# A list scheduler's model that books GpSimd and two-tensor VectorE steps as exclusive, with measured step lengths

## The chip, the cores and the metric

The kernel runs on one core of a Trainium2 chip. The metric is the time of one execution in microseconds, the median of several. Five engines matter. TensorE (PE in the profile; PEld is its weight load) does the matrix products, VectorE (DVE) and GpSimd (POOL) work element by element, ScalarE (ACT) does activations and scaled copies, and SyncE (SP) issues the DMAs. Matmul results land in PSUM banks; all else lies in SBUF.

## The reference

The input is one sequence of 512 tokens of width 2048 with a context of 256 tokens, all in float32. A first block normalizes both, projects them, and runs four attention mixers of four heads (A global, B neighbourhood, C window with sinks, D with low-rank keys and values). A second block has two layers: an even one (causal pooling, and an attention of 16 heads of 64 over the 128 best keys of each query) and an odd one (32 heads of 64 in a window, with sinks).

```python
# first block
h_x = rms_norm(x, norm_g) * (1 + sc_x) + sh_x
px, pc = split_cols(h_x @ w_in), split_cols(h_c @ w_in)
oa, ob, oc, od = mixer_a(...), mixer_b(...), mixer_c(...), mixer_d(...)
x = x + gt_x * (concatenate([oa, ob, oc, od]) @ w_out)
# even layer
h = rms_norm_2(x, norm_g) @ w_in
py = silu(p_gate) * (einsum(pooled, pool_w) * pool_scale)
o = dsa_attention(q, k, dv, iq, ik, iw, rel_bias, topk)   # score + bias, masked, softmax, @ v
x = x + concatenate([py, silu(d_gate) * o]) @ w_out
# odd layer
o = swa_sink_attention(q, k, v, sinks, rel_bias)
x = x + (silu(gate) * o) @ w_out
```

## The kernel before

Activations lie with the 2048 features in 16 tiles of 128 partitions and the tokens in the columns. Every weight and activation is split into a high part (ScalarE, a rounded copy) and a low part (what is left, by VectorE or GpSimd), and a product is three matmuls: high by high, high by low, low by high (L491 to L493, 512 columns each). Weights are streamed from HBM in units of 128 x 512: the load, the high part (L554), the low part (L564, a choice of VectorE or GpSimd) and the matmuls. So one tile of a projection is four units, 48 matmuls (16 feature tiles by three) into one PSUM tile `px`, with 512 tokens as columns.

All work is written as generators, and a list scheduler (`Sched`, L46 to L175) sets the order at build time. Each generator yields an engine and a cost before it issues an instruction. The scheduler keeps a clock for each engine, takes the pending step that could start first by these costs, and emits it. A list of two engines, as `[D(n), G(n, bias=SLACK)]`, leaves the choice to it: the one that would end first, GpSimd with a bonus. The costs are four one-line functions (`D`, `A`, `G`, `M`) and `DC`. What comes out is one fixed order of instructions for each engine. On the chip each engine runs its own list in order and waits only for data and buffers.

The projections have a low priority, so their matmuls fill the times in which attention waits. Where a layer ends, three steps meet. Outputs `o` of heads that were stored in DRAM are loaded again (`reload`, L970) and split at L291 (`o<-b`); the output projection (`out_proj`, L1560) starts its first tiles early, as far as outputs are ready; and the last head's softmax and product (PV) run. A softmax group computes scores `S` for 128 queries, VectorE scales them and adds a bias, ScalarE takes exponentials, the result `P` is scaled (L314 on VectorE or L312 on ScalarE), transposed on TensorE (`T`, L398), split into `pt`, and multiplied with the values.

Names that the steps below use: in the heads of the even and the odd layer (`pair64`, L1748) the bias sum L1803 (`P<-tab,sco` or `P<-tab,cmask`), the score matmuls L1809 and L1810, and the step L1815 that frees the one `S` bank; `rsqrt` (L347), whose last six steps (L363 to L365, twice) are small VectorE steps, booked as one; L412, the matmul of a head's statistics, ahead of those; L1704, which multiplies the result with a row statistic; L1902 and L1904, the PV products there; L1909 to L1921, from PV to the head's output `o`. In the first block, `attention` has the scores at L1113, the scaling of `S` into `P` at L1152, and `k` scaled at L846.

## Time and profile before

| | |
|---|---|
| median of 3 runs | 2746.86 us (2741.91 to 2751.96) |
| the profiled execution's own time | 2743.26 us |
| its span, first to last instruction | 2741.2 us |
| mean granted clock of TensorE | 0.988 |
| busy share of TensorE, VectorE, ScalarE, GpSimd | 97%, 54%, 42%, 40% |
| DMA | 315.98 MB, mean 115 GB/s |

The views are read like this. A wait row names the instruction that waited, what released it, the total wait, how often, and the longest. A timeline row has the start, the duration, the engine, the line, output and inputs, and in brackets how long the engine was idle before it. Engines overlap, so what matters is idle time of TensorE and matmuls at the lower clock (a matmul of 512 columns shows 0.39 us at the full clock, start to start 0.23, and 0.63 at the lower one).

### The profile page before, as it was taken

How to read it: one execution, taken by the hardware profiler on the slowest of the kernel's cores; microseconds unless marked ns; L12 is line 12 of the kernel's file. 1: busy time of each engine (PE TensorE's matmuls, PEld its weight loads, DVE VectorE, ACT ScalarE, POOL GpSimd, SP SyncE). 2: the span in 40 equal slices, each digit the busy share in tenths (PEclk: the TensorE clock that was granted, in tenths of full speed). 3: DMA queues.
4: the chain of work that ended last, by engine and by line, in shares of the span. 5: the costliest groups of instructions: out<-in, count | busy, mean ns of one | idle time of the engine just before them, and what ended most of it. 6: DMA issues, size and time to landing. Idle time of an engine off the chain costs nothing.

```text
span 2741.2 us, 36539 instructions
## 1 busy us (share of the span) xinstructions
PE 2659.6 (97%) x13324; PEld 2189.9 (80%) x13324; DVE 1471.3 (54%) x3242; ACT 1164.1 (42%) x2361; POOL 1098.7 (40%) x886
## 2 busy tenths in 40 slices
PE   7889999999999999999999999999999999999999
PEld 3468888888888887788888878777888888888887
DVE  2457753336552656522368576765215877777500
ACT  3444433333332455433442445454334555555421
POOL 1351333334333333344445544445444333344544
PEclk8989999999999999999999999999999999999999
DMA  9845542222221213244222322224442222222443
GB/s 348 301 166 182 171 144 75 76 72 74 70 71 61 70 65 112 88 144 144 85 85 93 108 85 87 90 78 142 148 140 91 94 87 99 90 80 85 143 139 126
DMA packets 121960, 315.98 MB, mean 115 GB/s; under 512 B 13874, under 2 KB 23986, under 8 KB 121780
## 3 DMA queue, kind: packets, MB, share of 16 engines
q1 hardware_dynamic: 121780, 313.65, 34.4%
q8 instruction: 104, 1.70, 0.3%
q14 instruction: 76, 0.62, 0.1%
HBM read 293.02 MB, written 32.11 MB: 119 GB/s over the span
## 4 chain that ended last, share of the span: by engine, by line
PE 80%; DVE 13%; DMA 2%; ACT 2%; issue 1%; POOL 1%; SPq 0%; DVEq 0%; POOLq 0%; ACTq 0%
PE px L491 20%; PE px L492 20%; PE px L493 20%; PE T L398 4%; PE S L1113 2%; PE pc L496 1%; PE pc L498 1%; PE pc L497 1%; DVE P L1803 1%; DVE P L1815 1%; PE T L412 1%; DVE P L314 1%; PE O L1088 1%; PE O L1089 1%; DVE sm L1820 1%
## 5 line engine op out<-in xcount | busy, mean ns | idle before, releaser
L564 POOL TENSOR_TENSOR w<-wr,w 128x512 fp32r<-128x512 f32 x696 | 919.5, 1322 | 1423.1 <-ACT w L554 1419.0
L554 ACT ACTIVATE w<-wr 128x512 fp32r<-128x512 f32 x736 | 463.2, 630 | 948.4 <-PE px L493 616.0
L491 PE MATMUL px<-u,w 128*128 128x512 f32 x1248 | 498.5, 399 | 0.0
L492 PE MATMUL px<-u,w 128*128 128x512 f32 x1248 | 488.8, 392 | 0.0
L493 PE MATMUL px<-u,w 128*128 128x512 f32 x1248 | 488.4, 391 | 0.0
L491 PE MATMUL px<-hx,w 128*128 128x512 f32 x816 | 331.9, 407 | 9.4 <-ACT w L554 6.3
L492 PE MATMUL px<-hx,w 128*128 128x512 f32 x816 | 323.2, 396 | 2.2 <-POOL hx L291 2.2
L493 PE MATMUL px<-hx,w 128*128 128x512 f32 x816 | 322.3, 395 | 1.7 <-POOL w L564 1.7
L491 PE MATMUL px<-o,w 128*128 128x512 f32 x752 | 295.0, 392 | 3.3 <-ACT o L288 3.3
L492 PE MATMUL px<-o,w 128*128 128x512 f32 x752 | 294.3, 391 | 0.5 <-DVE o L291 0.5
L493 PE MATMUL px<-o,w 128*128 128x512 f32 x752 | 294.0, 391 | 0.0
L493 PEld LDWEIGHTS px<-u,w 128*128 128x128 f32 x1248 | 234.8, 188 | 51.3
L491 PEld LDWEIGHTS px<-u,w 128*128 128x128 f32 x1248 | 236.1, 189 | 40.7 <-issue 0.3
L492 PEld LDWEIGHTS px<-u,w 128*128 128x128 f32 x1248 | 235.7, 189 | 39.6
L291 DVE TENSOR_TENSOR pt<-T,pt 128x512 fp32r<-128x512 f32 (+2 forms) x208 | 127.0, 616 | 111.7 <-ACT pt L288 110.3
L493 PEld LDWEIGHTS px<-hx,w 128*128 128x128 f32 x816 | 154.9, 190 | 38.7 <-POOL w L564 3.3
L491 PEld LDWEIGHTS px<-hx,w 128*128 128x128 f32 x816 | 155.7, 191 | 32.9 <-ACT w L554 9.0
L492 PEld LDWEIGHTS px<-hx,w 128*128 128x128 f32 x816 | 155.7, 191 | 19.8 <-POOL hx L291 2.7
L491 PEld LDWEIGHTS px<-o,w 128*128 128x128 f32 x752 | 142.2, 189 | 33.4 <-ACT o L288 4.0
L492 PEld LDWEIGHTS px<-o,w 128*128 128x128 f32 x752 | 142.1, 189 | 30.5 <-DVE o L291 1.1
L493 PEld LDWEIGHTS px<-o,w 128*128 128x128 f32 x752 | 142.0, 189 | 29.3
L1598 DVE TENSOR_TENSOR xr<-px,xr 128x512 f32<-128x512 f32 x32 | 22.1, 692 | 251.0 <-PE px L493 248.1
(343 smaller groups left out, 4365.2 us busy)
## 6 DMA issues: line engine op xcount, KB each, us to landing
wr<-w SPq DMA_DIRECT2D x237, 512.0 KB, 3.5
wr<-wout SPq DMA_DIRECT2D x89, 512.0 KB, 4.2
wr<-wada SPq DMA_DIRECT2D x37, 512.0 KB, 6.8
gw<-wada SPq DMA_DIRECT2D x64, 256.0 KB, 5.3
wr<-w SPq DMA_DIRECT2D x58, 256.0 KB, 4.0
wr<-wada SPq DMA_DIRECT2D x54, 256.0 KB, 6.0
x<-xr SPq DMA_DIRECT2D x32, 256.0 KB, 4.3
xr<-x SPq DMA_DIRECT2D x32, 256.0 KB, 4.5
```

The source lines that it names most:

```text
L291: eng.tensor_tensor(lo, src, f32(hi), op=OP.subtract)
L314: self.nc.vector.tensor_scalar(dst, src, col, None, op0=OP.mult)
L398: self.nc.tensor.transpose(p[:, j * 128:(j + 1) * 128], x, self.ident)
L412: nc.tensor.matmul(p[:, j * gq:(j + 1) * gq], sq[:, j * 128:(j + 1) * 128], self.ones[:, 0:1] if gq == 1 else self.halves, start=True, sto ...
L491: mm(px, hi[:, s], x[0], **kw)
L492: mm(px, hi[:, s], x[1], start=False, stop=False)
L493: mm(px, lo[:, s], x[0], **ke)
L496: mm(pc, lo[:, s], c[0], **kw)
L497: mm(pc, hi[:, s], c[0], start=False, stop=False)
L554: nc.scalar.activation(w[:, 0], r, AF.Copy)
L564: (nc.gpsimd if e == "POOL" else nc.vector).tensor_tensor(w[:, 1], r, f32(w[:, 0]), op=OP.subtract)
L1113: self.nc.tensor.matmul(o, l, r, start=i == 0, stop=i == len(ops) - 1)
```

## The change

The scheduler's model gets one more resource, `port`. A step whose cost is of the class `Port` can't start before the last such step has ended: all steps of GpSimd, VectorE steps with two operands in SBUF (`D2`, new), VectorE copies in the doubled mode (`x2`) and the small steps `DC`. The constants of the costs change: 0.13 instead of 0.075 us of fixed cost for VectorE, 0.19 instead of 0.1 for ScalarE, 0.15 instead of 0.1 for GpSimd, and 0.4427 ns a column for a matmul instead of 0.4167 and 3 ns. No instruction computes anything else than before; order and choice of engine follow from the costs. The lines move by 15 from L291 on (L291 is L306, L1815 is L1830).

```diff
-    def start(self, t, e):
+    def start(self, t, e, c):
         s = self.engine.get(e, 0.0)
+        if isinstance(c, Port):
+            s = max(s, self.port)
...
             self.engine[e] = end
+            if isinstance(c, Port):
+                self.port = end
...
+class Port(float):
+    pass
...
 def D(n=0, x2=False, k=1, ptr=0):
-    return ("DVE", k * (0.075 + n * (0.52e-3 if x2 else 1.04e-3) + 0.053 * ptr))
+    c = k * (0.13 + n * (0.52e-3 if x2 else 1.04e-3) + 0.053 * ptr)
+    return ("DVE", Port(c) if x2 else c)
+def D2(n=0, k=1, ptr=0):
+
+    return ("DVE", Port(D(n, k=k, ptr=ptr)[1]))
 def DC(k):
 
-    return ("DVE", 0.19 * k)
+    return ("DVE", Port(0.19 * k))
 def A(n=0, ptr=0, acc=0, k=1):
-    return ("ACT", k * (0.1 + n * 0.833e-3 + 0.093 * (ptr + acc)))
+    return ("ACT", k * (0.19 + n * 0.833e-3 + 0.093 * (ptr + acc)))
 def G(n=0, k=1, bias=0.0):
 
-    return ("POOL", k * (0.1 + n * 2.2e-3), bias)
+    return ("POOL", Port(k * (0.15 + n * 2.2e-3)), bias)
 def M(n, passes=1):
-    return ("PE", passes * (n * 0.4167e-3 + 0.003))
+    return ("PE", passes * (n * 0.4427e-3))
...
-            e = yield ([D(n), G(n, bias=SLACK)] if pool else D(n))
+            e = yield ([D2(n), G(n, bias=SLACK)] if pool else D(n))
...
-            e = yield [D(512), G(512, bias=WSLACK)]
+            e = yield [D2(512), G(512, bias=WSLACK)]
...
-                    e = yield [G(n), D(n)]
+                    e = yield [G(n), D2(n)]
```

Some thirty steps are marked in this way. What the order becomes is shown at three places.

VectorE in the second head of the even layer, from the end of its statistics (L1704, now L1719) to the release of the score bank (L1815, now L1830); `tab` and `sco` or `cmask` are the two parts of a bias. Before:

```order
L1704 TENSOR_TENSOR sm_13361<-sm_13361,rt 128x4 x2
L1803 TENSOR_TENSOR P_13433<-tab_13044,cmask 128x128
L1803 TENSOR_TENSOR P_13434<-tab_13044,sco_11354 128x256
L1803 TENSOR_TENSOR P_13433<-tab_13050,cmask 128x128
L1803 TENSOR_TENSOR P_13434<-tab_13050,sco_11354 128x256
L1803 TENSOR_TENSOR P_13435<-tab_13044,sco_11354 128x384
L1803 TENSOR_TENSOR P_13436<-tab_13044,sco_11355 128x512
L924 TENSOR_TENSOR gg_13459<-px_13316,rx 128x512
L1815 SCALAR_TENSOR_TENSOR P_13433<-S_13447,sm_13361,P_13433 128x128
L1803 TENSOR_TENSOR P_13437<-tab_13050,sco_11355 128x512
L1815 SCALAR_TENSOR_TENSOR P_13433<-S_13447,sm_13361,P_13433 128x128
```

Now:

```order
L1719 TENSOR_TENSOR sm_13333<-sm_13333,rt 128x4 x2
L1818 TENSOR_TENSOR P_13419<-tab_13063,cmask 128x128
L1818 TENSOR_TENSOR P_13419<-tab_13067,cmask 128x128
L1926 TENSOR_TENSOR o_13438<-O_13307,b_13437 64x512
L939 TENSOR_TENSOR gg_13449<-px_13280,rx 128x512
L1830 SCALAR_TENSOR_TENSOR P_13419<-S_13444,sm_13333,P_13419 128x128 x2
L1931 TENSOR_TENSOR o_13438<-pc_13327,b_13437 64x512
L1839 TENSOR_REDUCE sm_13466<-P_13419 128x1 x2
```

The sums of 256, 384 and 512 columns no longer stand ahead of the release, and a step of the previous head's output (L1926, once L1911) does. On TensorE, from the statistics (L412) to the second score group, there were 39, 39, 39, 39, 39, 42, 39 and 39 matmuls of projections in the eight heads; now there are 54, 45, 69, 54, 69, 36, 69 and 54. Of the 64 bias sums 15 were on GpSimd, and 32 are now.

VectorE at the end of the first block, the last `rsqrt` (L358 to L365, now L373 to L380) with the split of the last head's values `v` (L291, now L306). Before:

```order
L358 TENSOR_SCALAR sm_9618<-sm_9515 128x6
L291 TENSOR_TENSOR v_9602<-T_9603,v_9602 128x512
L363 TENSOR_TENSOR sm_9618<-sm_9514 128x6
L364 TENSOR_TENSOR sm_9618<-sm_9618 128x6
L365 SCALAR_TENSOR_TENSOR sm_9514<-sm_9618,sm_9514 128x6
L363 TENSOR_TENSOR sm_9618<-sm_9514 128x6
L364 TENSOR_TENSOR sm_9618<-sm_9618 128x6
L365 SCALAR_TENSOR_TENSOR sm_9514<-sm_9618,sm_9514 128x6
L291 TENSOR_TENSOR pt_9627<-T_9610,pt_9627 128x512
```

Now:

```order
L373 TENSOR_SCALAR sm_9608<-sm_9505 128x6
L1054 RECIPROCAL sm_9557<-sm_9557 128x1
L378 TENSOR_TENSOR sm_9608<-sm_9504 128x6
L379 TENSOR_TENSOR sm_9608<-sm_9608 128x6
L380 SCALAR_TENSOR_TENSOR sm_9504<-sm_9608,sm_9504 128x6
L378 TENSOR_TENSOR sm_9608<-sm_9504 128x6
L379 TENSOR_TENSOR sm_9608<-sm_9608 128x6
L380 SCALAR_TENSOR_TENSOR sm_9504<-sm_9608,sm_9504 128x6
L306 TENSOR_TENSOR v_9610<-T_9611,v_9610 128x512
L306 TENSOR_TENSOR pt_9635<-T_9618,pt_9635 128x512
```

The split of `v` has gone behind the six small steps, and the reloaded outputs' splits (`o<-b`) from VectorE to GpSimd, where seven stand in a row (five before).

TensorE in the same stage, at the score groups of the last head (`S<-kvc,qn` and the three rows behind it are one group). Before, the last group:

```order
L491 MATMUL pc_9905<-o_9688,w_9904 128x512
L492 MATMUL pc_9905<-o_9688,w_9904 128x512
L493 MATMUL pc_9905<-o_9688,w_9904 128x512
L1113 MATMUL S_9987<-kvc_9674,qn_9430 128x256 x3
L1113 MATMUL S_9987<-kc_9817,qr_8890 128x256 x2
L1113 MATMUL S_9987<-k_9673,qn_9430 128x512 x3
L1113 MATMUL S_9987<-ks_9816,qr_8890 128x512 x2
L491 MATMUL pc_9905<-o_9705,w_9904 128x512
L492 MATMUL pc_9905<-o_9705,w_9904 128x512
L493 MATMUL pc_9905<-o_9705,w_9904 128x512
L491 MATMUL px_9585<-o_9707,w_9948 128x512
```

Now, the first two groups:

```order
L506 MATMUL px_9586<-o_9787,w_9895 128x512
L507 MATMUL px_9586<-o_9787,w_9895 128x512
L508 MATMUL px_9586<-o_9787,w_9895 128x512
L1128 MATMUL S_9875<-kvc_9819,qn_9416 128x256 x3
L1128 MATMUL S_9875<-kc_9903,qr_8875 128x256 x2
L1128 MATMUL S_9875<-k_9818,qn_9416 128x512 x3
L1128 MATMUL S_9875<-ks_9902,qr_8875 128x512 x2
L1128 MATMUL S_9979<-kvc_9819,qn_9416 128x256 x3
L1128 MATMUL S_9979<-kc_9903,qr_8875 128x256 x2
L1128 MATMUL S_9979<-k_9818,qn_9416 128x512 x3
L1128 MATMUL S_9979<-ks_9902,qr_8875 128x512 x2
L1128 MATMUL S_9995<-kvc_9819,qn_9416 128x256 x3
```

The four groups now follow each other with no matmul of the output projection (`pc<-o`, `px<-o`) between them, and the transposes come right behind; before, 9, 12 and 12 of those matmuls stood between the groups and 12 behind the last.

TensorE at the end of the odd layer, behind the last PV product (L1904, now L1919). Before (`o_22726`, the last head's output, comes 63 matmuls behind the last L1904):

```order
L1902 MATMUL O_22562<-pt_22648,v_2771_17788 128x128
L1904 MATMUL O_22562<-pt_22648,v_2771_17788 128x128
L1902 MATMUL pc_22598<-pt_22648,v_2771_17788 128x128
L1904 MATMUL pc_22598<-pt_22648,v_2771_17788 128x128
L491 MATMUL px_22590<-o_22478,w_22535 128x512
L492 MATMUL px_22590<-o_22478,w_22535 128x512
L493 MATMUL px_22590<-o_22478,w_22535 128x512
L491 MATMUL px_22590<-o_22601,w_22535 128x512
L492 MATMUL px_22590<-o_22601,w_22535 128x512
```

Now, `o_22779` being the last head's output:

```order
L1917 MATMUL O_22655<-pt_22751,v_2772_17800 128x128
L1919 MATMUL O_22655<-pt_22751,v_2772_17800 128x128
L1917 MATMUL pc_22659<-pt_22751,v_2772_17800 128x128
L1919 MATMUL pc_22659<-pt_22751,v_2772_17800 128x128
L506 MATMUL px_22553<-o_22779,w_22684 128x512
L507 MATMUL px_22553<-o_22779,w_22684 128x512
L508 MATMUL px_22553<-o_22779,w_22684 128x512
L506 MATMUL px_22667<-o_22573,w_22706 128x512
L507 MATMUL px_22667<-o_22573,w_22706 128x512
```

The last output is used right behind the last PV; before, 63 matmuls stood between. GpSimd in that stage, before:

```order
L564 TENSOR_TENSOR w_22589<-wr_22476,w_22589 128x512
L291 TENSOR_TENSOR o_22601<-b_22582,o_22601 128x512
L564 TENSOR_TENSOR w_22652<-wr_22476,w_22652 128x512
L291 TENSOR_TENSOR o_22615<-b_22586,o_22615 128x512
L564 TENSOR_TENSOR w_22691<-wr_22554,w_22691 128x512
L291 TENSOR_TENSOR o_22621<-b_22595,o_22621 128x512
L564 TENSOR_TENSOR w_22714<-wr_22554,w_22714 128x512
L564 TENSOR_TENSOR w_22736<-wr_22671,w_22736 128x512
```

Now:

```order
L579 TENSOR_TENSOR w_22595<-wr_22462,w_22595 128x512
L306 TENSOR_TENSOR o_22562<-b_22545,o_22562 128x512
L306 TENSOR_TENSOR o_22564<-b_22546,o_22564 128x512
L306 TENSOR_TENSOR o_22566<-b_22547,o_22566 128x512
L306 TENSOR_TENSOR o_22569<-b_22548,o_22569 128x512
L579 TENSOR_TENSOR w_22634<-wr_22528,w_22634 128x512
L306 TENSOR_TENSOR o_22571<-b_22549,o_22571 128x512
L306 TENSOR_TENSOR o_22573<-b_22550,o_22573 128x512
L306 TENSOR_TENSOR o_22576<-b_22551,o_22576 128x512
L579 TENSOR_TENSOR w_22666<-wr_22528,w_22666 128x512
L306 TENSOR_TENSOR o_22611<-b_22602,o_22611 128x512
```

All eight reloaded outputs are split on GpSimd now, and three were before. Between the even and the odd layer 33 matmuls stood between the last PV and the last output, and 6 do now.

## Rows read from the trace of the kernel before

**Rows 1.** The page: busy time by engine; the granted TensorE clock in 40 slices

```profile
PE 2659.6 (97%) x13324; PEld 2189.9 (80%) x13324; DVE 1471.3 (54%) x3242; ACT 1164.1 (42%) x2361; POOL 1098.7 (40%) x886
...
PEclk8989999999999999999999999999999999999999
```

**Rows 2.** Waits of TensorE, 0 to 200 us (total us, times, longest us)

```profile
PE T L667 <- DMA wr<-wada: 16.3, 6, 7.1
```

**Rows 3.** Waits of TensorE, 1200 to 2741 us

```profile
PE S L1809 <- DVE P L1815: 14.9, 9, 3.0
...
PE px L491 <- ACT o L288: 1.9, 1, 1.9
```

**Rows 4.** Waits of TensorE, 1075 to 1150 us

```profile
PE T L398 <- DVE pt L291: 4.0, 3, 2.8
...
PE T L398 <- DVE v L291: 1.1, 1, 1.1
```

**Rows 5.** Window of the even heads: length, busy us by engine, clock, DMA

```profile
1540.00:1875.00 335.00, 319.99 (x1548) 264.77 (x1548) 247.82 (x499) 168.76 (x369) 154.43 (x131) 0.99 0.26 86
```

**Rows 6.** Timeline of the second even head: start, duration us, instruction, [idle before <-releaser]

```profile
1585.31 0.39 PE L491 MATMUL px<-u,w 128*128 128x512 f32 x1
...
1585.54 0.39 PE L492 MATMUL px<-u,w 128*128 128x512 f32 x1
...
1588.33 1.36 DVE L1704 TENSOR_TENSOR sm<-sm,rt 128x4 f32<-128x4 f32 x2
...
1590.35 1.48 DVE L1803 TENSOR_TENSOR P<-tab,sco 128x256 f32<-128x256 f32 x3
...
1593.73 0.38 PE L1809 MATMUL S<-k,q 128*128 128x256 f32 x1 [3.04 <-DVE P L1815]
...
1595.20 0.63 PE L491 MATMUL px<-u,w 128*128 128x512 f32 x1
...
1595.63 0.63 PE L492 MATMUL px<-u,w 128*128 128x512 f32 x1
```

**Rows 7.** Timeline of VectorE, 1083 to 1096 us, end of the first block

```profile
1085.53 0.68 DVE L291 TENSOR_TENSOR v<-T,v 128x512 fp32r<-128x512 f32 x1
...
1086.88 1.21 DVE L364 TENSOR_TENSOR sm<-sm 128x6 f32<-128x6 f32 x1
...
1091.81 0.17 DVE L365 SCALAR_TENSOR_TENSOR sm<-sm,sm 128x6 f32<-128x6 f32 x1
1091.89 0.68 DVE L291 TENSOR_TENSOR pt<-T,pt 128x512 fp32r<-128x512 f32 x1
```

**Rows 8.** Timeline of GpSimd in the same place

```profile
1085.55 6.21 POOL L291 TENSOR_TENSOR o<-b,o 128x512 fp32r<-128x512 f32 x5 [0.16 <-ACT o L288]
```

**Rows 9.** Timeline, 1131 to 1137 us, behind the last head's scores

```profile
1131.23 0.62 PE L1113 MATMUL S<-ks,qr 128*128 128x512 f32 x2
...
1131.90 1.02 DVE L1152 TENSOR_SCALAR P<-S,sm 128x768 f32<-128x768 f32 x1 [0.36 <-PE S L1113]
...
1135.38 0.62 DVE L314 TENSOR_SCALAR P<-P,sm 128x768 f32<-128x768 f32 x1
...
1136.06 0.77 PE L398 MATMUL T<-ident,P 128*128 128x128 f32 x5 [1.15 <-DVE P L314]
```

**Rows 10.** Timeline, 1893 to 1899 us, the even layer's last output

```profile
1893.23 0.27 PE L1904 MATMUL pc<-pt,v 128*128 128x128 f32 x1
...
1896.93 0.61 ACT L288 ACTIVATE o<-o 128x512 fp32r<-128x512 f32 x1
...
1897.57 1.37 DVE L291 TENSOR_TENSOR o<-o,o 128x512 fp32r<-128x512 f32 x1 [0.91 <-ACT o L288]
```

**Rows 11.** Timeline of GpSimd, 2552 to 2580 us, reloaded outputs

```profile
2564.63 1.29 POOL L291 TENSOR_TENSOR o<-b,o 128x512 fp32r<-128x512 f32 x1 [1.74 <-ACT o L288]
...
2567.58 1.75 POOL L291 TENSOR_TENSOR o<-b,o 128x512 fp32r<-128x512 f32 x1
```

**Rows 12.** Waits of TensorE, 2540 to 2741 us

```profile
PE T L398 <- DVE P L314: 0.2, 1, 0.2
```

More of the change, by code (lines that the diff above doesn't have):

```diff
@@ L75, in __init__ @@
         self.count = 0
+        self.port = 0.0
     def spawn(self, gen, prio=5):
@@ L155, in run @@
                     e, c = t.req[0][:2]
-                    s = self.start(t, e)
+                    s = self.start(t, e, c)
                     fixed.append((e, s, c))
@@ L164, in run @@
                     for e, c, *bias in t.req:
-                        s = self.start(t, e)
+                        s = self.start(t, e, c)
                         f = s + c - (bias[0] if bias else 0)
@@ L279, in spawn, with split @@
         self.s.spawn(gen, prio)
-    def split(self, hi, lo, src, g=None, pool=False, x2=False):
+    def split(self, hi, lo, src, g=None, pool=False, two=False):
         nc = self.nc
@@ L294, in split @@
             nc.scalar.activation(hi, src, AF.Copy, scale=g)
-            yield D(n, ptr=1)
+            yield (D2 if two else D)(n, ptr=1)
             nc.vector.scalar_tensor_tensor(lo, src, g, f32(hi), op0=OP.mult, op1=OP.subtract)
@@ L439, in rope @@
         u = yield from self.alloc("b")
-        yield D(n, ptr=1)
+        yield D2(n, ptr=1)
         nc.vector.scalar_tensor_tensor(dst, src, gain, cos, op0=OP.mult, op1=OP.mult)
@@ L690, in gate @@
                 c = self.csil[:, k:k + 1]
-                yield D(512, ptr=1)
+                yield D2(512, ptr=1)
                 if k == 0:
@@ L742, in stats @@
                 if i > 0:
-                    yield D(n)
+                    yield D2(n)
                     nc.vector.tensor_tensor(sums[0].val, sums[0].val, sums[i].val, op=OP.add)
@@ L825, in q_flow @@
         else:
-            yield from self.split(s[:, 0], s[:, 1], q, self.g(gname))
+            yield from self.split(s[:, 0], s[:, 1], q, self.g(gname), two=True)
             yield ev
@@ L838, in k_norm @@
         if ss_extra is not None:
-            yield D()
+            yield D2()
             nc.vector.tensor_tensor(ss[:, :6], ss[:, :6], ss_extra, op=OP.add)
@@ L928, in silu @@
         nc.scalar.activation(th, px, AF.Tanh, scale=0.5)
-        yield D(512)
+        yield (D2 if rstd is not None else D)(512)
         nc.vector.scalar_tensor_tensor(th, th, 1.0, px, op0=OP.add, op1=OP.mult)
@@ L1035, in soft @@
                 nc.scalar.activation(es, sink, AF.Exp, bias=nm)
-                yield D()
+                yield D2()
                 nc.vector.tensor_tensor(su, su, es, op=OP.add)
@@ L1602, in f @@
                     s = yield from self.pair("u")
-                    yield from self.split(s[:, 0], s[:, 1], xr, self.g(gname, c))
+                    yield from self.split(s[:, 0], s[:, 1], xr, self.g(gname, c), two=True)
                     self.s.set(u[c], (s[:, 0], s[:, 1]))
@@ L1701, in q64 @@
         yield from self.rsqrt(rs, ss, 1.0, EPS * 64)
-        yield D(k=2)
+        yield D2(k=2)
         for i in range(2):
@@ L1838, in soft @@
                 nc.scalar.activation(es, es, AF.Exp)
-                yield D()
+                yield D2()
                 nc.vector.tensor_tensor(su, su, es, op=OP.add)
@@ L1919, in pv_ @@
             th = gev.val
-            yield D(512)
+            yield D2(512)
             nc.vector.scalar_tensor_tensor(o, th, 0.5, o, op0=OP.mult, op1=OP.mult)
@@ L2003, in flow @@
                         count[j] += 1
-                        yield D(n, first)
+                        yield D2(n, first)
                         if first:
@@ L2025, in choose @@
             dg = w[:, j * 128:]
-            yield D(128)
+            yield D2(128)
             nc.vector.tensor_tensor(dg, dg, tri, op=OP.add)
@@ L2071, in flow @@
                 z = two[n % 2]
-                yield D(512)
+                yield D2(512)
                 nc.vector.scalar_tensor_tensor(z, s, 1.0 / w, x, op0=OP.mult, op1=OP.subtract)
                 e = yield from self.alloc("sm")
-                yield D(k=2)
+                yield D2(k=2)
                 nc.vector.tensor_tensor(e[:, :w], s[:, :w], self.rcnt[:, c // 2, :w], op=OP.mult)
```

24 lines of the change are left out of this document (12 added, 12 removed).

## The prediction

> **What bounds the kernel now.** I read the page's shares first: TensorE is busy 97% of the span and the granted clock is full in nearly every slice [rows 1]. No matmul is added or removed, so only idle TensorE time and time at the lower clock can change: 2741.2 - 2659.6 = 81.6 us of idle time, plus the slow stretches. The waits of TensorE, stage by stage, then say whose idle time that is. In the first 200 us it waits mostly for DMA (16.3 us for the modulation weights [rows 2]), and no order of VectorE and GpSimd changes when those bytes land. From 1200 us on one wait stands out: the even layer's score matmul L1809 waits for VectorE to release the only score bank, 14.9 us in 9 waits [rows 3]. At the end of the first block (1075 to 1150 us) the waits are for splits and small steps of VectorE, 4.0 us for split transposes and 1.1 us for a split v [rows 4]. The windows put the even layer's heads at 319.99 us busy of 335 [rows 5].
>
> The timeline of the second even head shows the exclusion that the change is about. A step of two SBUF tensors with 4 columns takes 1.36 us for two [rows 6] while GpSimd runs, and where GpSimd's five splits stand back to back for 6.21 us [rows 8], small steps that take 0.17 us take 1.21 us [rows 7]. The old costs book 0.19 us for such a step and let both engines run at once. So the order is planned on a VectorE that is faster than the real one, and the score bank is released late: 3.04 us of waiting in that head.
>
> **The change part by part.** It adds no instruction to TensorE; it changes the order and which engine takes a split, a bias sum or a scaling. I go by places.
>
> *Even layer, wait for the score bank.* What must be hidden is the chain from the statistics matmul to the second L1815, which releases the bank. In the second head it takes 39 matmuls of 512 columns at 0.227 us (start to start [rows 6]) plus the wait: 8.9 + 3.0 = 11.9 us. The orders give the cover: matmuls between the statistics and the second score group are 39 in seven heads and 42 in one before; now they are 54, 45, 69, 54, 69, 36, 69 and 54. With the chains of before, heads with 54 or more have 12.3 us or more of cover and wait no longer; the second has 10.2 us, but the wide bias sums that stood ahead of its release on VectorE, of which three took 1.48 us [rows 6], are gone from there, so I take no wait; the sixth has 8.2 us and four splits of transposes in its chain, so it still waits some 4 us. Of 14.9 us about 4 stay: -10.9. Bounds: none stays (-14.9); or the 17 bias sums more on GpSimd (15 before, 32 now), at 1.3 us for 512 columns as a split of that size takes [rows 11], hold VectorE back as before (-7).
>
> *Clock.* After the 3.04 us wait the clock drops to its lower level: seven matmuls of 0.63 us, 0.43 apart instead of 0.23 [rows 6], cost 7 x 0.2 = 1.4 us. Two of the nine waits are followed by such a stretch; I take one back: -1.4 (0 to -2.8).
>
> *End of the first block, first part.* Before, v's split comes ahead of the six small steps; it ran just before them, and the split of the transposes came behind at 1091.89 [rows 7]. Now v's split stands behind all six, and GpSimd has seven splits in a row, not five. TensorE's transposed-v work is covered by three matmuls only. v would come up to 1091.9 - 1086.2 = 5.7 us later, of which 2.8 us of the wait for the next split, which falls in the same time, is not paid twice: +3.0 (0 to 5.7).
>
> One rule of the Trainium skill ("SBUF — State Buffer", section "Who interferes with whom") speaks against the change here: the pair of ports that VectorE's second input shares with GpSimd is held by whoever issues first for one whole instruction. The change books six small steps as one hold of 1.14 us; by the rule GpSimd gets in between each two of them, and the trace agrees (at 1086.88 the second step is held for 1.21 us, and the last only begins at 1091.81 [rows 7], beside the 6.21 us of splits [rows 8]). By that the six take some 6 us with seven splits queued, by the booking 1.1 us, and +3.0 would be about 0.
>
> *End of the first block, second part.* The last head's four score groups had 9, 12 and 12 projection matmuls between them and 12 behind; now none. The bank is one: group, then L1152 of 1.02 us, then the next group. A group ends at about 1131.7, L1152 runs from 1131.90 to 1132.92 [rows 9], so each of three gaps is up to 1.3 us; and behind the last group the softmax chain to the scaled P is bare: 1131.7 to 1136.0 is 4.3 us, of which 1.15 was waited before. That is at most 3.9 + 3.2 = 7.1. But the 45 matmuls that left are executed somewhat earlier, where TensorE waited too [rows 4], so part comes back: I take +5 (2 to 7.1).
>
> *Even to odd layer.* From the last PV matmul (1893.5) the hi half of the last output takes to 1897.54 [rows 10]: 4.0 us. Before 33 matmuls cover it, now 6 (1.4 us); 2.6 us come bare, but a wait of 1.9 us for a reloaded output [rows 3] loses its place as 42 instead of 21 matmuls stand ahead of the transposes: +1 (-1 to 3).
>
> *Odd layer to the last projection.* Before, no wait at all worth the name [rows 12]: 63 matmuls between the last PV and the use of the last output. Now none: the whole 4.0 us to hi is bare, plus some 0.2 us to begin. All eight reloaded outputs are now split on GpSimd (three before), five of them in a stretch with only one weight split between. GpSimd gives one per 1.29 to 1.75 us [rows 11], TensorE uses one in three matmuls, 0.68 us; over four in a row 3 x (1.3 - 0.7) = 1.8. Sum +6 (4 to 11, the upper with 1.75 us each and weights' splits late behind them), and one stretch at the lower clock more, +1.4.
>
> *The rest.* Weight splits stay on GpSimd (696 before, 699 now) and are streamed ahead. The scalings moved from VectorE to ScalarE lie on an engine busy 42%. The first 1000 us keep nearly the same order of matmuls; I take 0, with 5 us either way for small shifts.
>
> Sum: -10.9 - 1.4 + 3.0 + 5 + 1 + 6 + 1.4 = +4.1. The profiled execution took 2743.26 us, so 2747.4 by it; the median of the runs is 3.6 us above that execution, so 2751.
>
> **Rivals.** Less than 0.3% (8.2 us) either way is what a measurement of this kernel can't tell from no change.
>
> *The score waits go, the boundaries cost little.* All 14.9 and 2.8 us are won; the projections that were drawn forward fill waits in the places from which the boundaries borrow, so the first block gives +2, the even layer -1, the last +4 as the lower bounds have it: -17.7 + 5 = -12.7, or 2734. For it: the waits at 1083 to 1093 us are there to be filled. Against: the chain behind the last PV can't be hidden without matmuls.
>
> *The boundaries decide.* The price is GpSimd's queue: seven and eight splits in a row in front of which VectorE's small steps stand, at 1.2 us each. From the point where a projection needs a new output every 0.68 us and GpSimd is the only supplier, TensorE goes at GpSimd's pace. Upper bounds of the first block and the last (5.7 + 7.1 + 11), +3 in the even layer, two slow stretches 2.8, against -7 of the score waits and nothing of clock: +22.6, or 2769; half way there it is 2760.
>
> *The change doesn't do what it says.* Nothing on the chip holds the two engines apart: no wait is added between GpSimd and VectorE, so they collide where their data happen to be ready, and the model's reservation is only an order. Then the score chains stay as long as now; the longer cover still works, but the second and the sixth head wait: -9 with no clock won, and the boundaries cost 16.4 as in the sum: +7.4, or 2754. It differs from the forecast in the durations, hardly in the time.
>
> **How the numbers follow.** The forecast's case, boundaries eating up what the score bank gives back, gets 0.40 with the third rival in it, with 2743 to 2758 as its own range; the first rival 0.29, the second 0.31. Faster by over 0.3% is the first rival: 0.29; slower is the second: 0.31; within 0.40. The range goes from 2730, a little under the first rival's time, to 2769, that of the second with its upper bounds.
>
> **What would show it.** Waits of the score matmul on VectorE in the even layer falling from 14.9 to about 4 us, one head carrying nearly all of it, would show the first step. Waits of TensorE at the end of the first block rising from about 9 to about 17 us, with the score matmuls of its last head among them, the second. A wait of about 4 us for the last output right behind the last PV matmul, and GpSimd's splits of reloaded outputs as what is waited for before it, the third. The prediction is wrong if the first 1000 us lose or gain more than 5 us, or if the boundaries show no new wait.

## The result, and the profile after

The changed kernel took 2720.44 us (median of 4, 2719.18 to 2721.56), the kernel before 2747.61 us in the same runs: a ratio of 0.9906, 95% interval 0.9892 to 0.9921. That is 27 us faster, where no measurable change was forecast (2751, range 2730 to 2769). The profiled execution spans 2718.9 us, 22.3 us less than before.

The page of the changed kernel, busy time by engine and the granted clock, against [rows 1]:

```profile
PE 2655.8 (98%) x13324; PEld 2192.5 (81%) x13324; DVE 1362.8 (50%) x3151; ACT 1194.6 (44%) x2415; POOL 1121.8 (41%) x923
...
PEclk8989999999999999999999999999999999999999
```

TensorE idles 63 us (2718.9 - 2655.8) instead of 82. Its waits from 1200 us on (total us, times, longest), against [rows 3]:

```profile
PE px L506 <- ACT o L303: 6.5, 3, 3.3
PE px L507 <- POOL o L306: 1.7, 4, 0.9
PE T L413 <- DVE b L1743: 1.6, 1, 1.6
```

The row of the score matmul is gone altogether: 14.9 us are 0. At its place stand the ends of the layers, waits for the last output and for reloaded ones. The window of the even heads has no idle time left, 377.00 us busy of 377 (columns as in [rows 5]):

```profile
1463.00:1840.00 377.00, 377.00 (x1834) 317.23 (x1833) 237.20 (x522) 189.82 (x400) 212.93 (x189) 1.00 0.29 96
```

To compare two orders, I lined up the two traces by TensorE's own work: its matmuls' columns at 0.4427 ns, 60 ns at least for a matmul, summed up in the order in which they run; both kernels come to 2505 us of it. A stage is a stretch of this sum, and the table gives how long each trace took for the same stretch (from start times of all matmuls; the head counts from the first matmul). The kernels of the experiments below stand in the same table.

| stage (us of work) | before | changed | e1 | e2 | e9 | e10 | e4 | e7 | e12 |
|---|---|---|---|---|---|---|---|---|---|
| head, 0 to 200 | 255.3 | 245.8 | 246.9 | 255.0 | 255.6 | 241.5 | 242.0 | 242.6 | 238.5 |
| first block, 200 to 950 | 809.2 | 801.9 | 802.9 | 808.7 | 807.1 | 800.8 | 802.3 | 801.7 | 802.8 |
| its end, 950 to 1030 | 102.5 | 109.0 | 104.9 | 102.1 | 100.3 | 99.9 | 101.1 | 103.3 | 96.4 |
| even layer, 1030 to 1330 | 307.0 | 308.1 | 307.5 | 308.3 | 314.1 | 305.0 | 308.2 | 306.6 | 307.4 |
| even heads, 1330 to 1680 | 388.0 | 365.9 | 366.0 | 389.6 | 389.0 | 366.1 | 365.9 | 365.9 | 366.0 |
| end of the even layer, to 1722 | 47.3 | 53.1 | 47.0 | 48.5 | 47.2 | 51.9 | 47.7 | 51.4 | 47.2 |
| odd layer, to 2300 | 613.9 | 608.2 | 610.4 | 613.8 | 614.9 | 607.6 | 611.6 | 608.4 | 610.4 |
| its end, to 2360 | 63.8 | 72.7 | 63.7 | 65.0 | 66.5 | 69.3 | 64.8 | 66.9 | 64.0 |

Behind 2360 every trace takes 145 us. Each column is one execution. How far such a stage varies by itself can be read where orders are equal: the head took 245.8, 242.0 and 242.6 us in the changed kernel, e4 and e7, 244.7 and 238.5 in e11 and e12, while the first block behind it agrees within 0.6 us in these groups. So 6 us in the head say nothing; elsewhere it is about 1 us, but more in the even heads where scores wait (see e3).

So the change won 9.5 us in the head, 7.3 in the first block, 22.1 in the even heads and 5.7 in the odd layer, and lost 6.5, 5.8 and 8.9 at the three ends. In the even heads 15.0 of the 22.1 us are idle time (15.0 before, 0 now) and 7.2 are matmuls that took longer around the waits. The granted clock accounts for 3.4 of these: before, it stood at the lower level (0.50) behind the waits of 3.04 and 2.37 us, for 6.8 us together, but not behind one of 3.00 us; now it doesn't fall there. The other 3.8 us fall at the full clock. The head has time at the lower clock as well, a mean granted clock of 0.90 before and 0.93 now, which is 51 and 34 us at half speed (columns as in [rows 5]). The kernel before, its head and the two stretches in the even heads:

```profile
0.00:260.20 260.20, 223.23 (x1092) 145.59 (x1093) 129.75 (x278) 104.07 (x194) 80.47 (x70) 0.90 0.73 254
...
1594.80:1598.20 3.40, 3.40 (x10) 2.72 (x9) 2.31 (x7) 2.42 (x10) 0.62 (x1) 0.50 0.50 158
1772.30:1775.70 3.40, 3.39 (x10) 2.91 (x11) 3.19 (x9) 1.43 (x7) 1.60 (x1) 0.51 0.11 46
```

The changed kernel's head:

```profile
0.00:250.80 250.80, 219.46 (x1092) 142.32 (x1093) 117.28 (x268) 103.78 (x193) 79.83 (x72) 0.93 0.73 254
```

The second even head, now without a wait (timeline of all engines, start and duration in us):

```profile
1572.62 0.16 DVE L378 TENSOR_TENSOR sm<-sm 128x8 f32<-128x8 f32 x1
...
1573.62 0.17 DVE L380 SCALAR_TENSOR_TENSOR sm<-sm,sm 128x8 f32<-128x8 f32 x1
...
1574.04 0.23 DVE L1719 TENSOR_TENSOR sm<-sm,rt 128x4 f32<-128x4 f32 x2
...
1575.97 1.70 POOL L1818 TENSOR_TENSOR P<-tab,sco 128x256 f32<-128x256 f32 x2
...
1578.12 0.22 PE L1824 MATMUL S<-k,q 128*128 128x128 f32 x1
...
1578.71 0.61 DVE L1830 SCALAR_TENSOR_TENSOR P<-S,sm,P 128x128 f32<-128x128 f32 x2 [0.39 <-PE S L1825]
...
1581.98 0.28 PE L1824 MATMUL S<-k,q 128*128 128x256 f32 x1
```

The six small steps take 1.2 us together (1572.62 to 1573.79; 5.2 us before). The two wide sums are on GpSimd, and ahead of the scores. The score group starts at 1578.12 and L1830, which frees the bank, follows 0.6 us later; the next group at 1581.98 waits for nothing. In the kernel before, the scores started at 1587.35 and the second L1815 ended 6.3 us behind that:

```profile
1587.35 0.22 PE L1809 MATMUL S<-k,q 128*128 128x128 f32 x1
...
1593.33 0.34 DVE L1815 SCALAR_TENSOR_TENSOR P<-S,sm,P 128x128 f32<-128x128 f32 x1
```

At the end of the first block the six small steps still meet the splits on GpSimd. VectorE, against [rows 7]:

```profile
1067.94 0.88 DVE L378 TENSOR_TENSOR sm<-sm 128x6 f32<-128x6 f32 x1 [0.30 <-ACT sm L375]
...
1069.25 0.17 DVE L378 TENSOR_TENSOR sm<-sm 128x6 f32<-128x6 f32 x1
...
1070.65 1.21 DVE L380 SCALAR_TENSOR_TENSOR sm<-sm,sm 128x6 f32<-128x6 f32 x1
1071.79 0.68 DVE L306 TENSOR_TENSOR v<-T,v 128x512 fp32r<-128x512 f32 x1
```

GpSimd, against [rows 8]:

```profile
1069.33 8.70 POOL L306 TENSOR_TENSOR o<-b,o 128x512 fp32r<-128x512 f32 x7 [0.53 <-ACT o L303]
```

The last score groups there have no projections between them (waits of TensorE in brackets, against [rows 9]):

```profile
1111.37 0.62 PE L1128 MATMUL S<-kvc,qn 128*128 128x256 f32 x3 [0.99 <-ACT P L1165]
...
1114.45 0.63 PE L1128 MATMUL S<-kvc,qn 128*128 128x256 f32 x3 [1.06 <-ACT P L1165]
...
1117.53 0.62 PE L1128 MATMUL S<-kvc,qn 128*128 128x256 f32 x3 [1.06 <-ACT P L1165]
...
1123.77 1.11 PE L413 MATMUL T<-ident,P 128*128 128x128 f32 x5 [2.76 <-DVE P L329]
```

And the two later ends. TensorE at the end of the even layer, waiting for a reloaded output (1.87 us before, [rows 3]) and then for the last one:

```profile
1848.76 0.49 PE L506 MATMUL px<-o,w 128*128 128x512 f32 x1 [1.21 <-ACT o L303]
...
1873.29 0.50 PE L506 MATMUL px<-o,w 128*128 128x512 f32 x1 [1.92 <-ACT o L303]
```

All engines at the end of the odd layer, GpSimd with four reloaded outputs in a row, and TensorE's wait for the last output:

```profile
2532.91 5.01 POOL L306 TENSOR_TENSOR o<-b,o 128x512 fp32r<-128x512 f32 x4
...
2534.24 0.50 PE L507 MATMUL px<-o,w 128*128 128x512 f32 x1 [0.87 <-POOL o L306]
```

```profile
2557.26 0.50 PE L506 MATMUL px<-o,w 128*128 128x512 f32 x1 [3.35 <-ACT o L303]
```

### The profile page after: what moved, and what is told of

The parts are those of the page before. It is cut to its first block, busy times and chain, and to the rows that moved or that the text cites. A ratio compares the mean times of both kernels' runs of the same rounds, so it can differ in the third digit from the quotient of the medians.

```text
span 2718.9 us, 36544 instructions
## 1 busy us (share of the span) xinstructions
PE 2655.8 (98%) x13324; PEld 2192.5 (81%) x13324; DVE 1362.8 (50%) x3151; ACT 1194.6 (44%) x2415; POOL 1121.8 (41%) x923
## 4 chain that ended last, share of the span: by engine, by line
PE 93%; DVE 2%; DMA 2%; ACT 1%; POOL 0%; issue 0%; SPq 0%; ACTq 0%; DVEq 0%; POOLq 0%
PE px L506 23%; PE px L507 23%; PE px L508 23%; PE T L413 4%; PE S L1128 2%; PE pc L511 2%; PE pc L513 1%; PE pc L512 1%; PE T L427 1%; DMA wr<-w 1%; PE S L1825 1%; PE T L682 1%; PE S L1824 1%; PE O L1103 1%; PE O L1104 1%; PE O L1102 1%
## 5 line engine op out<-in xcount | busy, mean ns | idle before, releaser
L306 DVE TENSOR_TENSOR pt<-T,pt 128x512 fp32r<-128x512 f32 (+2 forms) x208 | 127.7, 616 | 162.7 <-ACT pt L303 161.9
L506 PEld LDWEIGHTS px<-hx,w 128*128 128x128 f32 x816 | 155.4, 190 | 31.3 <-ACT w L569 6.2
L303 ACT ACTIVATE pt<-T 128x512 fp32r<-128x512 f32 (+2 forms) x208 | 110.1, 537 | 123.8 <-PE O L1104 57.3
```

The source lines that it names most:

```text
L303: nc.scalar.activation(hi, src, AF.Copy)
L306: eng.tensor_tensor(lo, src, f32(hi), op=OP.subtract)
L506: mm(px, hi[:, s], x[0], **kw)
```

## The experiments

The theories: E, that the exclusion of GpSimd and two-tensor steps carries the gain; L, that the longer steps do; B, that the ends lose because projections were used up too early; S, that they lose to GpSimd's queue of reloaded splits. The kernel before, run beside each of them, had medians of 2743.1 to 2745.3 us.

One booking of the change isn't what it should be. The step that adds up the index scores of the even layer (L2004, now L2019) was booked as `D(n, first)` and is now `D2(n, first)`: the second argument of `D` is `x2`, that of `D2` the factor `k`. `first` is false for 45 of these 48 steps, so the plan gives them no time at all, in the changed kernel and in every run but e8; in the trace of the changed kernel they take 0.65 us each, 29 us in all. e2 and e9 have the same booking and gain nothing, so it isn't what gains; what it costs the change was not measured.

**e1, the exclusion alone**

```diff
-    c = k * (0.13 + n * (0.52e-3 if x2 else 1.04e-3) + 0.053 * ptr)
+    c = k * (0.075 + n * (0.52e-3 if x2 else 1.04e-3) + 0.053 * ptr)
-    return ("ACT", k * (0.19 + n * 0.833e-3 + 0.093 * (ptr + acc)))
+    return ("ACT", k * (0.1 + n * 0.833e-3 + 0.093 * (ptr + acc)))
-    return ("POOL", Port(k * (0.15 + n * 2.2e-3)), bias)
+    return ("POOL", Port(k * (0.1 + n * 2.2e-3)), bias)
-    return ("PE", passes * (n * 0.4427e-3))
+    return ("PE", passes * (n * 0.4167e-3 + 0.003))
```

> The changed planner with the exclusion of GpSimd and two-tensor VectorE steps, but with the old step lengths (0.075, 0.1 and 0.1 us fixed, 0.4167 ns a column and 3 ns for a matmul). Theory E (the exclusion carries the gain; step lengths hardly matter): the score waits of the even heads fall from 15 to under 3 us, the first 1000 us gain some 15 us as in the changed kernel, and the time is 2715 to 2728. Rival L (the step lengths carry it, since they alone slow the planned VectorE against the planned TensorE everywhere): 2740 to 2750, even score waits still over 8 us. By the covers in its order (51, 69, 39, 66, 69, 39, 66, 39 matmuls against 39 before) I expect four heads without a wait, 2725.

Measured: 2703.55 us, ratio 0.9838 (0.9817 to 0.9858): faster than expected and 17 us faster than the whole change. Head, first block and even heads are as in the change; the ends of the even and the odd layer cost nothing (47.0 and 63.7 us). Theory E holds, and the new step lengths, added to the exclusion, make the kernel slower.

**e2, the step lengths alone**

```diff
 def D2(n=0, k=1, ptr=0):
-    return ("DVE", Port(D(n, k=k, ptr=ptr)[1]))
+    return D(n, k=k, ptr=ptr)        # DC, G and x2 likewise
```

> The changed planner with the new step lengths but without the exclusion. Theory E: about as before, 2743 to 2750, since the cover from the statistics to the second score group stays at 36 to 45 matmuls and the even score waits stay at 12 us or more. Rival L: 2720 to 2730.

Measured: 2743.65 us, ratio 0.9996 (0.9984 to 1.0008), no change. The score waits stay:

```profile
PE S L1836 <- DVE P L1842: 13.9, 7, 2.8
```

Theory L falls.

**e3, the new model in the head only**

```diff
+SWITCH = {160: False}    # from weight unit 160 on, no exclusion and the old lengths
```

> The changed planner up to weight unit 160 (about the first 200 us), the old model behind it; from there the order is that of the kernel before. Theory H (the head's new order is worth the 9.4 us that the two profiles differ by there): 2738, with the loss in the first 200 us of matmul work 9 us smaller than before and everything behind as before. Rival N (the head is bound by DMA and the two profiles differ there by chance): 2747, and the difference in the head under 3 us.

Measured: 2743.47 us, ratio 0.9992 (0.9982 to 1.0001). The total didn't show the gain, the stages did: the first 200 us of work took 242.7 us (255.3 before), which is theory H's 9 us and more. 8 us went again in the even layer's pooling stage (314.9 instead of 307.0), where the order came out differently and a pooling matmul waited 3.9 us for VectorE, and 4 in the even heads. Behind the head, the index scores booked at no time are the only cost in which e3's model differs from the kernel before, and they stand in that stage, so the 8 us come with them; e6 and e9, which have them too, came out at 314 as well, but e1 at 307.5. The 4 us in the even heads go with the clock: the waits are the same (15.0 us), but the granted clock stood at the lower level for 17 us there, 6.8 in the kernel before. That the head's gain is no chance is also seen from the other traces: 255.0, 255.6 and 256.1 us in e2, e9 and e8, without the exclusion of two-tensor steps, and 238 to 247 in all that have it there.

**e4, the old model at the three ends**

```diff
+SWITCH = {335: False, 375: True, 587: False, 612: True, 782: False}
```

> The changed planner, but with the old model (no exclusion, old lengths) at the ends of the three attention stages: units 335 to 375, 587 to 612, and from 782 on. The matmuls kept for the ends come back: 63, 9, 9, 12 around the last score groups of the first block and 24 behind them, 36 and 63 behind the last PV of the even and the odd layer (0, 6 and 0 in the changed kernel). Theory B (the losses at the three ends, 6.5 + 5.8 + 8.8 us by the two profiles, come from matmuls used up too early, and the gains elsewhere don't depend on it): waits at the ends as before, 2720 - 21 = 2700, 2697 to 2706. Rival S (the ends lose because GpSimd gets the reloaded outputs' splits or because the layer simply arrives there earlier): 2712 to 2720.

Measured: 2699.76 us, ratio 0.9828 (0.9811 to 0.9845), as theory B had it. The ends took 101.1, 47.7 and 64.8 us (109.0, 53.1 and 72.7 in the change), and the gains elsewhere stayed, but for 3.4 us of the odd layer (611.6). It changes the reloaded splits as well (15 on GpSimd, not 23), so it doesn't tell B from S by itself. At the end of the even layer S has no part: the changed kernel splits one of the eight reloaded outputs there on GpSimd and takes 53.1 us, e1 six of seven and takes 47.0. For the two other ends see e5, e7 and e10.

**e5, exclusion and new fixed costs, old matmul length**

```diff
-    return ("PE", passes * (n * 0.4427e-3))
+    return ("PE", passes * (n * 0.4167e-3 + 0.003))
```

> The changed planner with the exclusion and the new fixed costs of VectorE, ScalarE and GpSimd, but the old length of a matmul. Port only took 2703.6 us and the whole change 2720.4, and the 17 us lie at the three ends. Theory F (longer fixed costs make TensorE idle longer in the plan, so projections are drawn forward and are missing at the ends): its order keeps 0, 0, 0 and 0 matmuls at the last scores of the first block, 0 behind the last PV of the even layer and 30 behind that of the odd: 4 + 6 + 3 us on top of port only, 2712 to 2718. Rival M (the matmul's length is what does it): 2702 to 2707.

Measured: 2709.92 us, ratio 0.9878 (0.9863 to 0.9893). Between the two expected ranges, with theory F's sign: 53.4 us at the end of the even layer (47.0 in e1) and 76.5 at that of the odd (63.7), made up in part by a shorter head (238). The odd layer's end is the worst of all, although 30 matmuls stand behind its last PV. There all eight reloaded splits are in a row on GpSimd, the transposes wait for a softmax step of ScalarE, the small steps of the last softmax on VectorE (1.30 us below, for 2 columns) run beside the splits, and a projection waits for a split itself:

```profile
2517.91 9.85 POOL L318 TENSOR_TENSOR o<-b,o 128x512 fp32r<-128x512 f32 x8
...
2521.61 0.33 PE L425 MATMUL T<-ident,P 128*128 128x128 f32 x1 [4.13 <-ACT P L339]
...
2526.47 1.30 DVE L1854 TENSOR_TENSOR sm<-sm,vec 128x2 f32<-128x2 f32 x1
...
2529.03 0.79 PE L519 MATMUL px<-o,w 128*128 128x512 f32 x1 [2.19 <-POOL o L318]
```

So S has a part in it as well: the reloaded outputs, not the cover alone. The longest wait is not for GpSimd, though: ScalarE's step stands behind the high parts of seven reloaded outputs in its own queue.

**e6, exclusion and new matmul length, old fixed costs**

```diff
-    c = k * (0.13 + n * (0.52e-3 if x2 else 1.04e-3) + 0.053 * ptr)
+    c = k * (0.075 + n * (0.52e-3 if x2 else 1.04e-3) + 0.053 * ptr)
     # ACT and POOL as in e1, the matmul as in the change
```

> The exclusion and the new length of a matmul, with the old fixed costs. Its order keeps nothing at the last scores of the first block, but 51 and 45 matmuls behind the last PV of the even and the odd layer. Theory F: only the first block's end is dearer than in port only, by 4 us, so 2705 to 2710. Rival M: 2716 to 2721 as the whole change.

Measured: 2714.31 us, ratio 0.9890 (0.9875 to 0.9905), in neither range. The ends of the even and odd layer are free (44.6 and 64.3 us), as theory F says; the first block's end took 107.3 (104.9 in e1), and 6.7 us more were lost in the pooling stage (314.1, in e1 307.5), which neither theory had. The two later ends are as F has them; the total doesn't decide.

**e7, the change with reloaded outputs split on VectorE**

```diff
-                yield from self.split(s[:, 0], s[:, 1], t, pool=True)
+                yield from self.split(s[:, 0], s[:, 1], t, pool=False)
```

> The changed kernel with the low parts of reloaded outputs split on VectorE only. Theory B (cover): its order has 9, 9, 9 and 3 matmuls again around the last score groups of the first block, and 9 and 9 behind the last PV of the two layers, so the first end wins 4 us, the two others 1 to 2 each: 2713 to 2717. Rival S (GpSimd's pace with reloaded outputs is the loss at the last end): the 1.7 us waited for GpSimd's splits go and no more, with VectorE's small steps freed: 2717 to 2719.

Measured: 2702.16 us, ratio 0.9848 (0.9833 to 0.9863): much better than either had it. Of the 18 us to the change some 3 are the head, whose order is the same, so these say nothing; the first end gave 5.7, the last 5.8, the even one 1.7, and the pooling stage 1.5. At the first end the order brings 9, 9, 9 and 3 matmuls back, so B can explain it; at the last the cover is only 9, the wait for the last output fell from 3.35 to 1.73 us and the waits for GpSimd's splits went. The run changes cover and queue together, so it doesn't part them.

**e8, the kernel before with all bias sums on GpSimd**

```diff
-                    e = yield [G(n), D(n)]
+                    e = yield G(n)
```

> The kernel before, old model, with all 64 bias sums of the even heads on GpSimd. The cover from the statistics to the second score group stays at 39 to 45 matmuls. Theory C (the wide sums on VectorE are what makes the chain long, so the change won there by moving them): score waits fall from 15 to 5 us or less, 2730 to 2736. Rival Q (the place of the statistics and the small steps against GpSimd make it long; more work on GpSimd makes these worse): waits stay at 10 us or more, 2742 to 2752.

Measured: 2746.27 us, ratio 1.0011 (1.0001 to 1.0020). Theory C falls:

```profile
PE S L1809 <- DVE P L1815: 11.5, 6, 3.4
```

The small steps took 4.7 us in five heads and 2.9 in a sixth (5.2, 5.1 and 2.6 in three heads before), since GpSimd had more to do beside them. Moving sums without a plan that knows the collision moves the loss.

**e9, exclusion of the small steps alone**

```diff
 def D2(n=0, k=1, ptr=0):
-    return ("DVE", Port(D(n, k=k, ptr=ptr)[1]))
+    return D(n, k=k, ptr=ptr)        # x2 is free too, DC and G keep the exclusion; lengths as in e1
```

> The old step lengths, and the exclusion only between GpSimd and the small steps (DC); two-tensor steps of VectorE are free in the model. Theory P (the six small steps of a head's statistics beside GpSimd's splits are the part that the old plan gets wrong by most): the six steps take 1.2 to 2.2 us in nearly all even heads (up to 5.2 before), the longest score waits go and 4 to 8 us of the 15 stay, since the score matmuls still stand at 39 or so matmuls of cover: 2730 to 2736. Rival W (the exclusion of the wide two-tensor steps carries it): score waits of 10 us or more and 2740 to 2746, the rest of port only's 42 us coming from the wide steps.

Measured: 2748.79 us, ratio 1.0016 (1.0003 to 1.0029). Theory P falls. The six steps did shrink to 1.2 us in seven of eight heads, and 13.7 us of score waits stayed all the same. The second even head shows why (timeline of all engines; L1731 is L1704, L1830 the bias sum, L1842 the step that frees the bank):

```profile
1585.98 0.17 DVE L392 SCALAR_TENSOR_TENSOR sm<-sm,sm 128x8 f32<-128x8 f32 x1
...
1587.48 0.50 DVE L1731 TENSOR_TENSOR sm<-sm,rt 128x4 f32<-128x4 f32 x2
...
1589.10 1.74 POOL L591 TENSOR_TENSOR w<-wr,w 128x512 fp32r<-128x512 f32 x1
...
1589.61 3.08 DVE L1830 TENSOR_TENSOR P<-tab,sco 128x256 f32<-128x256 f32 x2
...
1590.69 0.22 PE L1836 MATMUL S<-k,q 128*128 128x128 f32 x1
...
1592.24 1.60 POOL L591 TENSOR_TENSOR w<-wr,w 128x512 fp32r<-128x512 f32 x1
...
1596.03 0.60 DVE L1842 SCALAR_TENSOR_TENSOR P<-S,sm,P 128x128 f32<-128x128 f32 x2
...
1596.69 0.39 PE L1836 MATMUL S<-k,q 128*128 128x256 f32 x1 [2.65 <-DVE P L1842]
```

The chain's other half, from L1731 at 1587.48 to the release at 1596.63, has the wide sums in it, and two of 256 columns take 3.08 us beside GpSimd (0.41 each alone). The scores start at 1590.69, in an order planned for a VectorE without that collision, and the next group waits 2.65 us. With the wide steps exclusive (e1), the sums stand ahead, on GpSimd, and the scores start just before VectorE can take them:

```profile
1571.56 0.17 DVE L392 SCALAR_TENSOR_TENSOR sm<-sm,sm 128x8 f32<-128x8 f32 x1
...
1574.78 1.72 POOL L1830 TENSOR_TENSOR P<-tab,sco 128x256 f32<-128x256 f32 x2
...
1576.21 0.22 PE L1836 MATMUL S<-k,q 128*128 128x128 f32 x1
...
1576.87 0.61 DVE L1842 SCALAR_TENSOR_TENSOR P<-S,sm,P 128x128 f32<-128x128 f32 x2 [1.13 <-PE S L1837]
```

**e10, the whole change without the small steps**

```diff
 def DC(k):
-    return ("DVE", Port(0.19 * k))
+    return ("DVE", 0.19 * k)
```

> The whole change but for the small steps, which are not exclusive in the model. Theory P: GpSimd stands beside the six steps again in some even heads, where they take 4 us or more; with 27 to 36 matmuls of cover in four heads score waits come back, 3 to 8 us and as much again in part by the clock; the first block's end wins some 5 us by its order (9, 9, 9 and 15 matmuls): 2716 to 2724. Rival W: the six steps stay short and no score wait comes back: 2711 to 2716.

Measured: 2698.51 us, ratio 0.9834 (0.9818 to 0.9851), 22 us better than the change (20 over the ratios). Rival W was nearer, and still too slow: no score wait came back, the small steps took at most 2.7 us, the first end took 99.9 us (9, 9, 9 and 15 matmuls kept), the last 69.3. So the exclusive small steps cost the change its cover at the first end and sent more reloaded splits to GpSimd there (14 of 14, 6 in e10), 9 us together, and the even heads are no faster for them (366.1 us without, 365.9 with). Some 4 us of the 22 are the head, which varies by more.

The last end parts B from S. e10 has no cover there either, the last output being used right behind the last PV, but only two of the eight reloaded splits are on GpSimd, and no matmul waits for one:

```profile
2530.48 0.27 PE L1931 MATMUL pc<-pt,v 128*128 128x128 f32 x1
...
2534.05 0.80 PE L518 MATMUL px<-o,w 128*128 128x512 f32 x1 [3.29 <-ACT o L315]
```

It takes 69.3 us, where e1, with cover, takes 63.7 and the change, with all eight splits on GpSimd, 72.7. So of the 9 us that the change lost there, 5.6 go with the missing cover (B) and 3.4 with the queue (S).

**e11 and e12, combinations**

```diff
+LONG = i < 160              # new lengths in the first 160 units, old ones behind, exclusion everywhere
+SWITCH = {335: False, 375: True}                       # e11 only
+yield from self.split(..., t, pool=False)              # reload, e12 only
```

> The exclusion everywhere but at the end of the first block (units 335 to 375, old model), the new step lengths in the first 160 units only. By stages of the runs so far: 242 us of the first 200 of matmul work, 101 at the end of the first block, 366 in the even heads, 47 and 64 at the two other ends, so 2693 to 2698, ahead of port only (2703.6) by the head (5 us) and the first end (4 us). If stages don't add up (later stages depend on how the earlier ones end), 2699 to 2705.

> As e11_mix, but with the exclusion also at the end of the first block, and reloaded outputs split on VectorE only. Theory: cover of 9, 9, 9 and 24 matmuls there and no queue of splits on GpSimd, so the first end takes 101 to 103 us and the two others 47 to 50 and 64: 2693 to 2699. Rival (VectorE with 24 more splits delays the softmax chains at the ends): 2700 or more.

Measured: e11 2699.06 us, ratio 0.9834 (0.9819 to 0.9849), e12 2694.84 us, ratio 0.9815 (0.9801 to 0.9830). For e11 the stages didn't quite add up: its first end took 103.5 instead of 101 (the head's 244.7 instead of 242 is less than equal orders differ by). e12 came in range, with 96.4 us at the first end, the best of all and below the 101 to 103 expected; its profile is of its fastest execution (2688.83 us). It beats both kernels, by 49 us and (over the ratios, 0.9815 against 0.9906) by 25.

## Why the prediction was wrong, point by point

The sum was +4.1 us, the traces differ by -22.3. By the table, 26 us of error are:

*"The first 1000 us keep nearly the same order of matmuls; I take 0."* This step failed, by 16.8 us up to 950 (9.5 in the head, 7.3 behind), and more than 5 us was the prediction's own sign of being wrong. Its premise doesn't hold: by line and tile names, about 83% of the first block's matmuls stand in the same order in both traces, 85% in the even heads, where I expected the change to act. And I didn't look at what the matmuls wait for. In e1 the same gain comes with the exclusion alone, in e2 and e9 it is absent: it comes with two-tensor steps of VectorE kept apart from GpSimd in the plan (e9 frees the copies in the doubled mode too, so these are not told apart). In the first block 5.8 of the 7.3 us are idle time of TensorE (7.7 before, 1.9 now), 2.1 of it one wait for the last step of a rotation (L448), which e2 and e9 still have with 1.8 and 2.1. In the head idle time went from 37.0 to 31.3 us and the time at the lower clock from 51 to 34; which of its short waits each step removes was not told apart.

*The score waits, -10.9, and the clock, -1.4.* The mechanism was named rightly, the size was not: -22.1. Two errors. First, I kept "the chains of before" and counted only projection matmuls as cover, so the sixth head, with 36 of them, was to wait 4 us. What counts is how far the scores stand ahead of the release. Over the eight heads that was 4.2 to 6.3 us before, and is 1.2 to 2.5 in the change and 1.2 to 1.3 in e1 (4.0 to 6.8 in seven heads of e2, 2.9 to 6.0 in e9). In all traces no head with up to 3.4 us waits and every one from 3.9 us on does, whatever the cover: one with 27 matmuls doesn't wait (e10), one with 51 does (e9). In the change the sixth head starts its scores 9.3 us behind its statistics and frees the bank at 10.8, with transposes and PV matmuls of the head before in the gap, which I hadn't counted. Second, the longer matmuls around nine waits cost 7.2 us (23.1 and 15.9 us above the sum of work), of which I took back 1.4, for one of the two stretches at the lower clock. Both went, with 3.4 us by the granted clock; the other 3.8, at the full clock, I hadn't in the sum.

*The odd layer, 0.* It gained 5.7 us, 2.5 of them idle time. The granted clock was full in both traces (1.00), so the other 3.2 us are matmuls that start later without an idle engine to be seen; their cause stays open.

*End of the first block, +3.0 and +5.* Together +6.5, so nearly right, but by luck, since the parts were not. In the first, the waits for v and for split transposes fell from 5.1 us (1.1 and 4.0, [rows 4]) to 1.3, a gain of 3.8 where I had a loss of 3.0; v's split was waited for 0.65 us. The six steps took 3.9 us (1067.94 to 1071.86), since GpSimd's seven splits began at 1069.33 only; of the four steps before that the first took 0.88 us, beside a weight split, and three took 0.17. The second part came as named, three waits of about 1.0 us between the groups and 0.9 and 2.76 behind them, 6.8 together where 1.15 was waited before: +5.6. And 3.4 us came from the clock, which the sum didn't have here (17 us at the lower level, 10 before).

On the rule of the Trainium skill ("SBUF — State Buffer", section "Who interferes with whom") that the shared pair of ports is held for one instruction at a time: the trace agrees where the two really meet, the last two steps at 1.16 and 1.21 us beside the splits. The six steps took 3.9 us here, between the 6 of the rule and the 1.1 of the booking, since four of them came ahead of the seven splits. In the even heads the plan kept GpSimd away from the six steps, all eight times.

*Even to odd layer, +1.* It was +5.8: waits of 1.21 and 1.92 us for outputs, where one of 1.87 stood before, and 3.4 us by the granted clock, which fell to the lower level twice (none before) and which I had left out here.

*Odd layer to the last projection, +6 and +1.4.* +8.9, right in kind: 3.35 us for the last output behind the last PV, 1.7 us in four waits for GpSimd's splits, 1.7 us by one stretch at the lower clock (for which I had 1.4); the rest was not told apart.

*The third rival, "nothing on the chip holds the two engines apart".* It fell. No wait was added, yet the order was enough for the six small steps, which take 1.2 us in all eight heads of the change. In e1 they take 1.8 to 2.2 in five heads, so planned gaps aren't always kept, and no score waits there either. Why they are kept as well as they are was not tested. The first rival (2734) had the right sign and the score waits right, all gone; its ends cost +5 and came to +21.2, and it left out the first block.

*The measured lengths.* I took the change as one. e1 and e2 part it: the exclusion is worth some 42 us, the lengths nothing alone, and together with the exclusion they cost 17: by the table 19 at the three ends, with 2 back in the odd layer. What the ends lack is the matmuls that were kept for them (e4, e10), and at the first and the last end GpSimd's queue of reloaded splits adds to it (e5, e7, e10). That the planner spends them early because its chains of VectorE are longer is argued from the orders, not shown. That it isn't chance that the score waits went is seen in the even heads: every order with the exclusion of two-tensor steps took 366 to 368 us there, every one without 388 to 392.

## What to carry to other kernels

When a planner sets the order, compare what is waited for, not only the order on the busiest engine: an order of matmuls taken for nearly equal hid 17 us. A resource that two engines share belongs in the plan, here for the two-tensor steps; how far an issue stands ahead of the step that frees its buffer shows whether the plan is right. A plan with longer steps draws filler work forward, so look at what filler is left where the chains at the end of a layer run bare. Time each part of such a change alone, and print what each step is booked at: 45 steps booked at nothing went unseen.

## What was not expected of the hardware

Two sums of 256 columns on VectorE took 3.08 us beside GpSimd (0.41 us each alone), and GpSimd's split beside them 1.74 instead of 1.29. Waits of TensorE of 1 to 3 us cost more than their own time: 15.0 us of idle time went together with 7.2 us of longer matmuls in the even heads, 3.4 by the granted clock and 3.8 at the full clock. Whether the clock fell behind such a wait differed between traces: with the same waits in the even heads, it stood at the lower level for 6.8 us in the kernel before and for 17 us in e3, and the stage took 388.0 and 392.0 us.
